# Which engine makes the low parts and scales the softmax rows in two attention stretches

## The chip, the cores and the metric

The kernel runs on one core of a Trainium2 chip. The metric is the device time of one execution in microseconds (us). Engines are called as the profile calls them: PE (TensorE, matmuls), PEld (its weight loads), DVE (VectorE), ACT (ScalarE), POOL (GpSimd), SP (SyncE, which issues most DMAs).

## The reference

Two layers of an encoder over 512 tokens of width 1024, all in float32. Each layer adds to x, in this order, half a gated SwiGLU feed-forward (FFN), a gated mixer, and half a second FFN, each behind an RMS norm with shift and scale from a conditioning vector. The mixer is

```
proj = h @ w_in              # q, k, v of branches A and C, u of B, forget logits, 3 x 1024 gates
ya = attention(qa, ka, va) + learned bias by relative distance, chunk-causal   # 8 heads of 64
yb = (trailing-window means of u - u) @ w_pool * pool_scale                      # windows 2, 4, 8, 16
yc = attention(qc, kc, vc) + cumulative log-forget bias, causal                # 8 heads of 64
out = (sum over n of sigmoid(g_n) * (y_n @ w_branch[n])) @ w_out
```

Softmax is over the keys; q and k are RMS-normalised per head.

## The kernel before, in words

Everything is kept transposed: features on 128 partitions, the 512 tokens along the free dimension. To keep float32 accuracy out of TensorE's faster format (`fp32r`), each operand is split in two: a high part `hi`, which is ScalarE's cast of the value, and a low part `lo`, which is the value minus `hi`. A product is then three matmuls (`triple`, lines 116 to 122): hi by hi, hi by lo, lo by hi.

Weights come in chunks of 512 KB. `wchunk` (from line 241) issues the DMA into `raw` (two buffers), lets ScalarE cast it to `whi` (line 268), and lets VectorE or GpSimd subtract to make `wlo` (line 270; three buffers each). Which engine it is hangs on `lo_share`: where `lo_share[0]` is 0, it is VectorE; where it is n, every n-th chunk goes to GpSimd. The mixer sets it to `LO_SHARE`, which is 1, ahead of branch A's attention and to 0 after branch C's, so that all 48 chunks of these stretches (12 in each of two stretches, in each of two layers) have their low parts made on GpSimd.

The two attention stretches of a layer are written by hand as an interleaving. `attention` walks over 8 heads and, in each, over the 4 blocks of 128 queries. For block i of a head

- `logits` makes the logits of the 128 (i + 1) keys that may be seen (lines 771, 772); VectorE adds the bias strip and takes the maximum (line 775, into a `t1` tile, of which there are two); ScalarE makes the exponentials and their sum (line 779, into one of three `t2` tiles); VectorE takes the reciprocal (line 781) and scales the row (line 782);
- `turn` transposes the scaled row in pieces of 128 on TensorE (line 794); ScalarE casts the high part (line 798) and VectorE makes the low part (line 799);
- `weigh`, once for two blocks, multiplies by v (lines 816, 817), ScalarE and VectorE add the two halves (lines 820, 821, in a `t1` tile), and `split_to` splits the result into the high and low parts of y (lines 370, 371), 64 partitions by 256 columns.

A small planner sets the order: `pe` counts the matmuls issued so far, in units of one matmul of 512 columns; `later(LAG_T, ...)` queues a block's transposes 24 units after its logits, and `later(LAG_V, ...)` queues the weighting 14 units after the last transposes. Between blocks a filler supplies other matmuls, up to a budget of 9.5 or 9 units: in branch A's stretch these are the q, k and v projections of branch C, in branch C's stretch the first merge, which multiplies branch A's y by its weights. So y of branch A is read in branch C's stretch, and y of branch C after it, behind the first product of a gate.

The bias strips (two buffers) are made a head at a time. In branch A a DMA brings the strip, and GpSimd overwrites a corner (line 746). In branch C two DMAs bring it out of DRAM, and GpSimd adds the causal mask to four blocks of 128 columns (line 757), the last of them in a separate tile `ssum` with one buffer. Besides, GpSimd normalises half the rows of q and k (line 659) and clears halves of q's tiles (line 677).

Each engine takes its instructions in order. The order within an engine follows the program's, but the framework that builds the kernel may put an instruction ahead of another that it holds to be ready later.

Of the kernel before, what the change touches and what calls it, by code (L numbers as in the profile page):

```python
# [15 lines left out]
F32 = mybir.dt.float32  # L16
# [3 lines left out]
ALU = mybir.AluOpType  # L20
# [11 lines left out]
NT = T // P  # L32
# [8 lines left out]
def encoder_kernel(tc, xT, c, w_ada, b_ada, gains, w_gate, w_up, w_down, w_qkv, w_f, w_ubg,  # L41
                   qk_gain, rel, fbias, w_pool, pool_scale, w_branch, w_out, inv_cnt, w_first, out):
    nc = tc.nc
# [20 lines left out]
    def st(shape, dt, tag, bufs):  # L64
        return sb.tile(shape, dt, tag=tag, bufs=bufs, name=nm(tag))
# [4 lines left out]
    def mmt(shape=(P, T)):  # L70
        return ps.tile(list(shape), F32, tag="mm", bufs=4, name=nm("mm"))

    def blk(tag, dt=F32R):
        bufs = {"xv": 4, "v2": 4, "b": NB}[tag]
        return st([P, 2, T], dt, tag, bufs)

    def t1(cols=T):
        return st([P, cols], F32, "t1", 2)

    def t2(cols=T):  # L80
        return st([P, cols], F32, "t2", 3)
# [16 lines left out]
    def later(delay, fn, group=None):  # L98
        t = Task(pe[0] + delay, fn, group)
        tasks.append(t)  # L100
        return t

    def poll(everything=False, group=None):
        if polling[0]:
            return
        polling[0] = True
        while True:
            ready = [t for t in tasks if t.fn is None or everything or t.due <= pe[0]
                     or (group is not None and t.group == group)]
            if not ready:  # L110
                break
            t = min(ready, key=lambda z: z.due)
            tasks.remove(t)
            t.run()
        polling[0] = False
# [250 lines left out]
            for d in range(KD):  # L366
                later(STEP * d, lambda d=d: self.pieces[hs].pop(0)() if len(self.pieces[hs]) == KD - d else None)

    def split_to(hi, lo, src):
        nc.scalar.copy(hi, src)  # L370
        nc.vector.tensor_tensor(lo, src, hi.bitcast(F32), op=ALU.subtract)  # L371


    def k_outer(chunk_src, nch, lhs_rhs, before_last=None):
# [57 lines left out]
    class Ffn:  # L432
# [19 lines left out]
        def act(self, n, pg, pu):  # L452
            sg = t1(T)
            nc.scalar.activation(sg, pg, AF.Silu)
            pr = t2(T)
            nc.vector.tensor_tensor(pr, pu, sg, op=ALU.mult)  # L456
            a = blk("b")
            split_to(a[:, 0, :], a[:, 1, :], pr)
            return a
# [164 lines left out]
    def proj_v(l, col, tag, res):  # L624
        vt = [None] * NT

        def evac(t, a):
            b = st([P, H, 2, HD], F32R, tag, 4)
            a3 = a.rearrange("p (h d) -> p h d", h=H)
            for odd in range(2):  # L630
                hi, lo = b[:, odd::2, odd, :], b[:, odd::2, 1 - odd, :]
                split_to(hi, lo, a3[:, odd::2, :])
            vt[t] = b

        yield from proj(l, col, evac)
        res.extend(vt)
# [65 lines left out]
    def finish_turns(upto=3):  # L702

        for todo in turns:
            while len(todo) >= 4 - upto:
                todo.pop(0)()


    def forget(l):
        raw = st([P, KD, H], F32, "wf", 1)  # L710
        nc.sync.dma_start(raw, w_f[l])
        f2 = st([P, KD, 40], F32R, "ssum", 1)
        nc.gpsimd.memset(f2.bitcast(F32), 0.0)
        split_to(f2[:, :, :H], f2[:, :, 32:32 + H], raw)
        pf = mmt()
        for k in range(KD):
# [26 lines left out]
    def strip_a(l, h):  # L743
        s = st([P, 768], F32, "strip", 2)
        nc.sync.dma_start(s[:, :T], rel[l, h])
        nc.gpsimd.memset(s[0:64, T - 64:T], NEG)
        return [s[:, T - (i + 1) * P:T] for i in range(NT)]
# [12 lines left out]
    def attention(qs, ks, vs, strip, ys, filler, budget, group):  # L760


        open_pt = {}

        def logits(h, i, strips):
            p, off = divmod(h, 2)
            (q, ql), k = qs[p], ks[p]
            odd = h % 2
            n = (i + 1) * P
            s = mmt()  # L770
            mm(s[:, :n], q[:, odd, i * P:(i + 1) * P], k[:, odd, :n], start=True, stop=False)
            mm(s[:, :n], ql[:, odd, i * P:(i + 1) * P], k[:, odd, :n], start=False, stop=True)
            lg = t1(T)[:, :n]
            mx = st([P, 1], F32, "mx", 4)
            nc.vector.tensor_tensor_reduce(out=lg, in0=s[:, :n], in1=strips[i], scale=-1.0, scalar=BIG,
                                           op0=ALU.add, op1=ALU.min, accum_out=mx)
            pr = t2(T)[:, :n]
            sm = st([P, 1], F32, "sm", 4)
            nc.scalar.activation(pr, lg, AF.Exp, bias=mx, scale=-1.0, accum_out=sm)
            rs = st([P, 1], F32, "rs", 4)  # L780
            nc.vector.reciprocal(rs, sm)
            nc.vector.tensor_scalar(pr, pr, rs, None, op0=ALU.mult)
            pe[0] += 0.5 * (i + 1.5)
            later(LAG_T, lambda: turn(h, i, pr), group)

        def turn(h, i, pr):
            half, c = divmod(i, 2)
            nj = 2 * half + 2
            if c == 0:
                open_pt[h] = st([P, 2, nj, 256], F32R, "ptb" if half else "pta", 2 if half else 1)  # L790
            pt = open_pt[h]
            tp = mmt()
            for j in range(i + 1):
                nc.tensor.transpose(tp[:, j * P:(j + 1) * P], pr[:, j * P:(j + 1) * P], ident)
            tv = tp[:, :(i + 1) * P].rearrange("p (j q) -> p j q", q=P)
            dh = pt[:, 0, :i + 1, c * P:(c + 1) * P]
            dl = pt[:, 1, :i + 1, c * P:(c + 1) * P]
            nc.scalar.copy(dh, tv)
            nc.vector.tensor_tensor(dl, tv, dh.bitcast(F32), op=ALU.subtract)
            pe[0] += 0.55 * (i + 1)  # L800
            if c == 1:
                later(LAG_V, lambda: weigh(h, half, pt), group)

        def weigh(h, half, pt):
            p, off = divmod(h, 2)
            rows = slice(off * HD, off * HD + HD)
            other = slice(HD - off * HD, 2 * HD - off * HD)
            if off == 0 and half == 0:
                ys.append(blk("b"))
            y = ys[p]  # L810
            o = mmt((P, HALF))
            nj = 2 * half + 2
            for j in range(nj):
                q0 = P if j == nj - 1 else 0
                v2 = vs[j][:, h, :, :].rearrange("p a d -> p (a d)")
                mm(o[:, q0:], v2, pt[:, 0, j, q0:], start=(j == 0), stop=False)  # L816
                mm(o[:, q0:], v2, pt[:, 1, j, q0:], start=False, stop=(j == nj - 1))  # L817
            cols = slice(half * HALF, (half + 1) * HALF)
            yl = t1(T)[:, :HALF]
            nc.scalar.copy(yl[rows, :], o[other, :])  # L820
            nc.vector.tensor_tensor(yl[rows, :], o[rows, :], yl[rows, :], op=ALU.add)
            split_to(y[rows, 0, cols], y[rows, 1, cols], yl[rows, :])
            pe[0] += 1.0 * nj

        for h in range(H):
            strips = strip(h)
            if group == "c":
                finish_turns(h // 2)
            for i in range(NT):
                logits(h, i, strips)  # L830
                if i == NT - 1:
                    heads[0] = h + 1
                poll()
                goal = pe[0] + budget
                while filler is not None and pe[0] < goal:
                    if next(filler, "end") == "end":
                        filler = None
                poll()
        if filler is not None:
            for _ in filler:  # L840
                pass
# [82 lines left out]
    class Mixer:  # L924
# [10 lines left out]
        def run(self, nxt):  # L935
# [14 lines left out]
            def fill_a():  # L950
                yield from proj_qk(l, 3, g8[:, 2:3], True, qc)
                yield from proj_qk(l, 4, g[:, 3:4], False, kc)
                yield from proj_v(l, 5, "v2", vc)
                yield from forget(l)

            lo_share[0] = LO_SHARE
            attention(qa, ka, va, lambda h: strip_a(l, h), ya, fill_a(), FILL_A, "a")
# [62 lines left out]
                    residual_tail(d, hs, o, modc[:, l, 5, d:d + 1], nxt)  # L1020

    FILL_A, FILL_C = 9.5, 9.0
    LO_SHARE = 1

    phases = []
    for l in range(L):
# [64 lines left out]
```

## Time and profile before

| what | value |
|---|---|
| median of 3 runs | 2480.24 us (2478.81 to 2480.9) |
| the profiled execution, span from first to last instruction | 2478.9 us |
| mean granted TensorE clock | 0.998 |
| attention A and C, layer 0 | about 460 to 585 and 585 to 675 us |
| attention A and C, layer 1 | about 1690 to 1810 and 1810 to 1900 us |
| instructions of PE, DVE, ACT, POOL | 11898, 2474, 1634, 327 |

The profiled execution's span lies inside the spread of the three runs, 1.3 us below their median. A row of a group reads: line, engine, operation, output<-inputs, shapes, count | busy us, mean ns of one | idle us before it <- what ended that. A row of the waits reads: who <- for whom: us in total, times, longest. A row of the timeline reads: start, length, engine, line, operation, count, and in brackets the idle time before it. "L782" is line 782.

### The profile page before, as it was taken

The page shows a single profiled execution, that of the slowest core. Times are in us where ns is not written, and L with a number is a line of the kernel's source. Part 1 is how long each engine was busy: PE and PEld are TensorE (multiplying, and loading weights), DVE is VectorE, ACT ScalarE, POOL GpSimd, SP SyncE. Part 2 cuts the span into 40 slices and gives each one's busy share as a digit, 9 for nine tenths or more (in the row PEclk, how much of TensorE's full clock was granted, in tenths as well). Part 3 has the DMA queues.
Part 4 walks back from the last instruction along what each step waited for, and adds up shares of the span by engine and source line. Part 5 has one row for each costly group of instructions (what it writes and reads, how often), then busy time and mean ns, then how long its engine had stood idle before and what let it go on. Part 6 is the DMA issues. An engine that isn't in the chain of part 4 may idle for free. (4 is left out here: it accounts for less than half of the span.)

```text
span 2478.9 us, 30855 instructions
## 1 busy us (share of the span) xinstructions
PE 2425.1 (98%) x11898; PEld 2030.1 (82%) x11898; DVE 1372.2 (55%) x2474; ACT 979.9 (40%) x1634; POOL 340.5 (14%) x327
## 2 busy tenths in 40 slices
PE   7999999999999999999999999999899999999999
PEld 5888888777788898888898888977778888888888
DVE  8655536788753365555365533377787434533332
ACT  5322235676532342222343223366765334432221
POOL 2000002343322200000000000124332322000000
PEclk9999999999999999999999999999999999999999
DMA  7655542222323435555335533322233233223322
GB/s 270 222 198 187 195 136 86 85 73 93 109 90 111 136 110 189 185 204 184 123 109 197 187 119 94 128 92 90 62 107 100 92 119 128 77 94 97 99 94 94
DMA packets 116263, 320.02 MB, mean 129 GB/s; under 512 B 11122, under 2 KB 13298, under 8 KB 116116
## 3 DMA queue, kind: packets, MB, share of 16 engines
q1 hardware_dynamic: 114962, 313.86, 37.9%
q0 software_dynamic: 1152, 4.19, 0.4%
q8 instruction: 93, 1.52, 0.3%
q14 instruction: 54, 0.44, 0.1%
q10 hardware_dynamic: 2, 0.00, 0.0%
HBM read 311.64 MB, written 6.38 MB: 128 GB/s over the span
## 5 line engine op out<-in xcount | busy, mean ns | idle before, releaser
L268 ACT CAST whi<-raw 128x1024 fp32r<-128x1024 f32 (+1 forms) x395 | 411.8, 1045 | 1077.3 <-PE acc L120 412.0
L270 DVE TENSOR_TENSOR wlo<-raw,whi 128x1024 fp32r<-128x1024 f32 x339 | 418.7, 1238 | 516.4 <-ACT whi L268 504.3
L121 PE MATMUL mm<-hhi,wlo 128*128 128x512 f32 x1304 | 507.4, 389 | 0.4 <-DVE wlo L270 0.4
L119 PE MATMUL mm<-hhi,whi 128*128 128x512 f32 x1304 | 507.6, 389 | 0.0
L120 PE MATMUL mm<-hlo,whi 128*128 128x512 f32 x1304 | 507.3, 389 | 0.0
L119 PE MATMUL acc<-b,whi 128*128 128x512 f32 (+1 forms) x960 | 355.9, 371 | 0.0
L121 PE MATMUL acc<-b,wlo 128*128 128x512 f32 (+1 forms) x960 | 353.5, 368 | 0.0
L120 PE MATMUL acc<-b,whi 128*128 128x512 f32 (+1 forms) x960 | 353.4, 368 | 0.0
L121 PEld LDWEIGHTS mm<-hhi,wlo 128*128 128x128 f32 x1304 | 244.8, 188 | 51.4 <-DVE wlo L270 0.9
L119 PEld LDWEIGHTS mm<-hhi,whi 128*128 128x128 f32 x1304 | 245.1, 188 | 50.9
L120 PEld LDWEIGHTS mm<-hlo,whi 128*128 128x128 f32 x1304 | 244.8, 188 | 50.8
L197 DVE CUSTOM_DVE_ANT_0 v<-v,b,badac 128x1024 f32<-128x1024 f32 x144 | 189.2, 1316 | 37.0 <-DMA v<-in_w_ada_dram 36.6
L121 PEld LDWEIGHTS acc<-b,wlo 128*128 128x128 f32 x960 | 181.0, 189 | 29.7
L120 PEld LDWEIGHTS acc<-b,whi 128*128 128x128 f32 x960 | 181.1, 189 | 29.3 <-DVE b L371 0.3
L119 PEld LDWEIGHTS acc<-b,whi 128*128 128x128 f32 x960 | 181.0, 189 | 28.8
L119 PE MATMUL acc<-hhi,whi 128*128 128x512 f32 x480 | 192.3, 402 | 1.7 <-ACT hhi L558 1.7
L121 PE MATMUL acc<-hhi,wlo 128*128 128x512 f32 x480 | 189.7, 395 | 0.6 <-POOL wlo L270 0.5
L120 PE MATMUL acc<-hlo,whi 128*128 128x512 f32 x480 | 188.9, 394 | 1.0 <-DVE hlo L561 1.0
L456 DVE TENSOR_TENSOR t<-mm,t 128x512 f32<-128x512 f32 x86 | 59.4, 691 | 202.7 <-PE mm L121 201.6
L270 POOL TENSOR_TENSOR wlo<-raw,whi 128x1024 fp32r<-128x1024 f32 (+1 forms) x56 | 132.9, 2376 | 170.9 <-ACT whi L268 136.4
L119 PE MATMUL acc<-whi,hhi 128*128 128x512 f32 x336 | 138.3, 412 | 4.9 <-ACT t L648 3.7
L120 PE MATMUL acc<-wlo,hhi 128*128 128x512 f32 x336 | 132.3, 394 | 0.0
(231 smaller groups left out, 3416.8 us busy)
## 6 DMA issues: line engine op xcount, KB each, us to landing
v<-in_w_ada_dram SPq DMA_DIRECT2D x144, 512.0 KB, 4.6
raw<-in_w_down_dram SPq DMA_DIRECT2D x88, 512.0 KB, 3.7
raw<-in_w_up_dram SPq DMA_DIRECT2D x82, 512.0 KB, 3.5
raw<-in_w_gate_dram SPq DMA_DIRECT2D x79, 512.0 KB, 3.6
raw<-in_w_ubg_dram SPq DMA_DIRECT2D x56, 512.0 KB, 3.5
raw<-in_w_qkv_dram SPq DMA_DIRECT2D x42, 512.0 KB, 3.8
raw<-in_w_branch_dram SPq DMA_DIRECT2D x24, 512.0 KB, 3.7
raw<-in_w_out_dram SPq DMA_DIRECT2D x16, 512.0 KB, 3.7
```

The lines of the kernel that those rows point to most:

```text
L119: mm(o, lh, rh, start=start, stop=False)
L120: mm(o, lh, rl, start=False, stop=False)
L121: mm(o, ll, rh, start=False, stop=stop)
L197: dot = nc.vector.tensor_tensor_reduce(out=raw, in0=raw, in1=silc[0], scale=1.0, scalar=badac[:, l, j, d:d + 1], op0=ALU.mult, op1=ALU.add ...
L268: nc.scalar.copy(hi, raw)
L270: lo_eng.tensor_tensor(lo, raw, hi.bitcast(F32), op=ALU.subtract)
L456: nc.vector.tensor_tensor(pr, pu, sg, op=ALU.mult)
```

## The change

In the two attention stretches the low parts of all weight chunks are made on VectorE (`LO_SHARE` is 0, so `lo_share` stays off). The softmax rows of 128, 256 and 384 columns are scaled on GpSimd; those of 512 columns stay on VectorE. The low parts of y in `weigh` are made on GpSimd; the other uses of `split_to` keep VectorE.

```diff
-    def split_to(hi, lo, src):
+    def split_to(hi, lo, src, lo_eng=nc.vector):
         nc.scalar.copy(hi, src)
-        nc.vector.tensor_tensor(lo, src, hi.bitcast(F32), op=ALU.subtract)
+        lo_eng.tensor_tensor(lo, src, hi.bitcast(F32), op=ALU.subtract)
...
             nc.vector.reciprocal(rs, sm)
-            nc.vector.tensor_scalar(pr, pr, rs, None, op0=ALU.mult)
+            (nc.vector if i == NT - 1 else nc.gpsimd).tensor_scalar(pr, pr, rs, None, op0=ALU.mult)
...
-            split_to(y[rows, 0, cols], y[rows, 1, cols], yl[rows, :])
+            split_to(y[rows, 0, cols], y[rows, 1, cols], yl[rows, :], nc.gpsimd)
...
-    LO_SHARE = 1
+    LO_SHARE = 0
```

## The prediction

> **What bounds the kernel now.** I read the page first, then busy time by stretch, then what TensorE waited for, then single collisions in the timeline. The page has the span and each engine's share:
>
> ```profile
> span 2478.9 us, 30855 instructions
> ...
> PE 2425.1 (98%) x11898; PEld 2030.1 (82%) x11898; DVE 1372.2 (55%) x2474; ACT 979.9 (40%) x1634; POOL 340.5 (14%) x327
> ```
>
> TensorE is idle for 2478.9 - 2425.1 = 53.8 us in all, so no change that leaves the matmuls alone can bring more than about 2%. Where is that idle time? The rows by stretch give start and end, length, and then the busy time of PE, PEld, DVE, ACT and POOL. The first two are attention A and attention C of layer 0, the next two those of layer 1, the last is a stretch of FFN:
>
> ```profile
> 460.00:585.00 125.00, 116.07 (x589) 92.24 (x588) 96.33 (x248) 86.83 (x185) 48.80 (x37) 0.99 0.26 80
> 585.00:675.00 90.00, 83.85 (x453) 68.72 (x452) 72.61 (x192) 56.21 (x142) 32.78 (x40) 0.98 0.33 106
> 1690.00:1810.00 120.00, 109.91 (x567) 87.50 (x568) 93.01 (x240) 81.89 (x178) 45.51 (x36) 1.00 0.27 81
> 1810.00:1900.00 90.00, 84.74 (x460) 69.97 (x459) 72.00 (x195) 57.43 (x143) 32.85 (x41) 0.98 0.34 110
> 850.00:1250.00 400.00, 400.00 (x2039) 343.06 (x2039) 220.35 (x354) 128.62 (x179) 17.62 (x17) 1.00 0.46 161
> ```
>
> The FFN stretch has no idle time on TensorE at all. The attention stretches have 8.93 + 6.15 + 10.09 + 5.26 = 30.4 us of it in 425 us, and VectorE is busy there for 333.95 us, 78.6%. What TensorE waited for, summed over the program (total, times, longest):
>
> ```profile
> PE mm L794 <- DVE t L782: 7.2, 7, 2.1
> PE mm L817 <- DVE ptb L799: 5.3, 5, 1.2
> ...
> PE acc L121 <- POOL wlo L270: 0.5, 1, 0.5
> ```
>
> The largest is the transposes of the softmax rows (L794) waiting for the scaling of the rows (L782); then the weighted sums waiting for VectorE's low parts of the transposed rows. GpSimd's low parts of the weight chunks make TensorE wait hardly ever (0.5 us). But see what they do to VectorE. Three rows of the timeline (start, length), GpSimd, VectorE and TensorE:
>
> ```profile
> 606.98 2.35 POOL L270 TENSOR_TENSOR wlo<-raw,whi 128x1024 fp32r<-128x1024 f32 x1
> ...
> 607.19 2.43 DVE L782 TENSOR_SCALAR t<-t,rs 128x512 f32<-128x512 f32 x1
> ...
> 609.68 0.66 PE L794 MATMUL mm<-ident,t 128*128 128x128 f32 x4 [2.10 <-DVE t L782]
> ```
>
> The scaling starts while GpSimd works on a chunk's low part, ends only after it, at 609.62, and the transposes behind it stand still for 2.10 us. The same scaling takes 0.48 us elsewhere (below). So the two engines exclude each other for such operations, and the 2.4 us pieces on GpSimd are paid on VectorE, on the path to TensorE.
>
> **The change part by part.** VectorE's groups, and three single undisturbed instructions:
>
> ```profile
> L270 DVE TENSOR_TENSOR wlo<-raw,whi 128x1024 fp32r<-128x1024 f32 x339 | 418.7, 1238 | 516.4 <-ACT whi L268 504.3
> ...
> L371 DVE TENSOR_TENSOR b<-t,b 64x256 fp32r<-64x256 f32 x64 | 36.6, 572 | 11.1 <-ACT b L370 9.9
> L782 DVE TENSOR_SCALAR t<-t,rs 128x512 f32<-128x512 f32 x32 | 30.6, 956 | 0.8
> ...
> L782 DVE TENSOR_SCALAR t<-t,rs 128x384 f32<-128x384 f32 x32 | 18.9, 592 | 0.8
> L782 DVE TENSOR_SCALAR t<-t,rs 128x128 f32<-128x128 f32 x32 | 18.8, 586 | 0.8
> ...
> L782 DVE TENSOR_SCALAR t<-t,rs 128x256 f32<-128x256 f32 x32 | 11.8, 370 | 0.7
> ```
>
> ```profile
> 478.81 0.41 DVE L371 TENSOR_TENSOR b<-t,b 64x256 fp32r<-64x256 f32 x1
> ...
> 598.84 0.48 DVE L782 TENSOR_SCALAR t<-t,rs 128x512 f32<-128x512 f32 x1
> ...
> 599.98 0.28 DVE L782 TENSOR_SCALAR t<-t,rs 128x128 f32<-128x128 f32 x1
> ```
>
> The groups of 128 columns average 586 ns, more than those of 256 (370): that is no price of the work but of collisions. And GpSimd's groups:
>
> ```profile
> L270 POOL TENSOR_TENSOR wlo<-raw,whi 128x1024 fp32r<-128x1024 f32 x48 | 115.8, 2417 | 136.4 <-ACT whi L268 110.6 <-PE acc L119 17.6 <-issue 8.0
> ...
> L315 POOL TENSOR_TENSOR ssum<-ssum,t 128x256 f32<-128x256 f32 x30 | 22.1, 738 | 98.7 <-ACT t L314 98.6
> L757 POOL TENSOR_TENSOR strip<-strip,cmask 128x128 f32<-128x128 f32 x48 | 21.8, 481 | 76.2 <-DMA strip<-fv_dram 64.1 <-DVE mx L775 8.2 <-DVE pta L799 4.0
> ...
> L160 POOL TENSOR_SCALAR_AFFINE_SELECT cmask<-cmask 128x128 f32<-128x128 f32 x1 | 0.3, 293 | 0.0
> ...
> L159 POOL MEMSET cmask<- 128x128 f32 x1 | 0.2, 204 | 0.0
> ```
>
> *Chunk low parts to VectorE.* 48 x 1.238 = +59.4 us on VectorE, -115.8 us on GpSimd. Each is done 1.2 us sooner once started, and releases its raw buffer sooner; no DMA holds TensorE in the stretches, so that is worth nothing by itself.
>
> *Rows of 128, 256 and 384 columns to GpSimd.* VectorE loses 18.8 + 11.8 + 18.9 = 49.5 us. On GpSimd no such scaling stands in the trace. Upper end: its two-input form, 0.481 us at 128 columns, 0.738 at 256, and by the same slope 0.995 at 384: 2.21 us a head, 71 us for 32 heads. Lower end: the memset's 0.204 us at 128 columns, scaled alike, 0.94 us a head, 30 us. I take the row that is likest, one input, one output, 0.293 us at 128: 0.293 / 0.481 of the upper end, so 0.29, 0.45 and 0.61 us, 1.35 us a head, 43 us. [...]
>
> *Low parts of y to GpSimd.* VectorE loses 36.6 us. GpSimd gains 64 x 0.738 = 47 us (two inputs, 256 columns; half the partitions, which I take not to shorten it). The merges that read y come a stretch later for branch A, and behind a gate's product for branch C; that cover hides some 0.3 us more each. If it were gone the price would be 64 x 0.33 = 21 us. One thing isn't covered by that: the source of y's low part is one of two `t1` buffers which the logits also use, so a late GpSimd would hold up the next logits on VectorE.
>
> *VectorE in sum.* +59.4 - 49.5 - 36.6 = -26.7 us. The 512-column rows stay on VectorE and now pay 32 x (0.956 - 0.48) = 15.2 us in collisions. GpSimd's longest new piece is about 0.74 us where it was 2.4, so I leave a third of that: -10 us more. VectorE's busy time in the four stretches goes from 334 to about 297 us, 78.6% to 69.9%. GpSimd goes to 340.5 - 115.8 + 43 + 47 = 315 us, no bound.
>
> *TensorE's idle time.* Of the 7.2 us behind L782, a 2.4 us blockade shrinks to at most 0.74: I take off 5 us. The other 30.4 - 7.2 = 23.2 us are waits for a VectorE that runs late in its queue. I let them shrink as queueing does, with busy / (1 - busy): 0.786 / 0.214 = 3.67 becomes 0.699 / 0.301 = 2.32, 37% less, 8.6 us. That is an estimate; its bounds are 0 and 23.2.
>
> *What is added.* A GpSimd stage between VectorE's reciprocal and the transposes. How much room is there? A VectorE scaling and its transposes in branch C, and a tight one (the scaling at 599.98 above):
>
> ```profile
> 625.53 0.35 DVE L782 TENSOR_SCALAR t<-t,rs 128x256 f32<-128x256 f32 x1
> ...
> 628.68 0.38 PE L794 MATMUL mm<-ident,t 128*128 128x128 f32 x2
> ...
> 600.52 0.27 PE L794 MATMUL mm<-ident,t 128*128 128x128 f32 x1
> ```
>
> The first ends at 625.88, 2.80 us before it is needed; the second at 600.26, 0.26 us before. Most rows have 2 to 4 us of room, and a longer scaling costs nothing there. I count 20 of the 96 as tight and 0.15 us each, +3 us; below that 0, above it the first rival.
>
> Sum: -5 - 8.6 + 3 = -10.6 us on the profiled span, 2478.9 to 2468.3. The profiled execution lies 1.3 us under the median of the runs, 2480.24, so the forecast is 2469.6 us.
>
> **The rivals.**
>
> *The same exclusion the other way round.* GpSimd now has short urgent work, VectorE long pieces:
>
> ```profile
> 745.71 2.37 POOL L971 TENSOR_TENSOR xv<-xv,t 128x512 f32<-128x512 f32 x1 [6.90 <-DVE t L970]
> ...
> 745.70 1.23 DVE L270 TENSOR_TENSOR wlo<-raw,whi 128x1024 fp32r<-128x1024 f32 x1
> ```
>
> GpSimd's sum starts with VectorE's chunk and ends 2.37 us later, 1.14 us of which remain after VectorE is done: it waited out the chunk. If all 20 tight scalings met a chunk, that is 20 x 1.23 = 25 us against the 13.6 us won: +11, 2491 us. Past 11 meetings (13.6 / 1.23) it is a loss. Against it: 12 chunks of 1.24 us are 15 us of a stretch of 90 to 125 us, so a scaling meets one about one time in seven. Chance 0.07. [...]
>
> *GpSimd's queue stands behind a bias strip.* GpSimd takes its instructions in order, and in branch C it masks each head's strip, which waits for a DMA:
>
> ```profile
> POOL strip L757 <- DMA strip<-fv_dram: 37.3, 7, 8.2
> ...
> 617.50 1.49 POOL L757 TENSOR_TENSOR strip<-strip,cmask 128x128 f32<-128x128 f32 x3 [7.57 <-DMA strip<-fv_dram]
> ```
>
> 37.3 us in 7 waits is 5.3 us each. If a row's scaling is queued behind such a wait, 5.3 - 2.8 = 2.5 us reach TensorE; for 7 heads in each of two layers 35 us, less the 10.6 won: 2504 us. It decides when more than 4 heads are hit so. For it: the order of a queue is made anew when the program is built (at 606.98 above a chunk's low part stands between mask adds that the code issues in a row). Against it: a strip is fetched two heads ahead, so the rows in flight were issued before it. Chance 0.07.
>
> *No change.* A VectorE queue that is stopped by other things:
>
> ```profile
> POOL wlo L270 <- ACT whi L268: 48.2, 9, 12.7
> ```
>
> In the first stretch GpSimd stood 48.2 us waiting for the high parts from ScalarE, at no cost. VectorE takes over that wait, and behind it stand the logits, the low parts of the transposed rows, the reciprocals. If 0.2 to 0.3 us of it are lost on each of 48 chunks, 10 to 14 us, the gain is gone: 2476 to 2484 us. For it: every wait of VectorE lies on TensorE's path. Against: where a chunk stands in the queue is chosen by when its high part should be ready. Chance 0.18.
>
> **How the numbers follow.** Forecast 0.68, no change 0.18, the two slower ones 0.07 each. A measurement of this kernel can tell about 0.2%, 5 us. Low end: three quarters of the 30.4 us gone, 2457. High end: the no-change case, 2484. Beyond lie the slower rivals and little else. Faster 0.68, same 0.18, slower 0.14.
>
> **What would show it.** Right: PE idle in the four stretches near 20 us; VectorE's 512-column scalings below 0.7 us on average; VectorE busy near 297 us there; GpSimd's scalings near 0.3, 0.45 and 0.6 us; no row "PE mm L794 <- POOL t L782" above some 3 us. Wrong: that row large, with GpSimd's own idle time ended by a strip's DMA (the queue) or its scalings stretched beyond 1 us (the exclusion); or logits waiting for VectorE chunks. A gain far above 11 us would mean that idle time was VectorE's lateness nearly alone.

## The result and the profile after

The changed kernel takes 2472.67 us (median of 7 runs, 2471.66 to 2472.94), the kernel before beside it 2480.18 us (7 runs, 2477.77 to 2481.32). The ratio is 0.9973 [0.9962, 0.9983]: 7.5 us or 0.3% faster. The forecast was 2469.6.

The page of the changed kernel:

```profile
span 2470.9 us, 31073 instructions
...
PE 2424.9 (98%) x11898; PEld 2028.9 (82%) x11898; DVE 1328.2 (54%) x2362; ACT 981.6 (40%) x1634; POOL 377.3 (15%) x439
```

The span is 8.0 us shorter. TensorE's busy time is the same (2425.1 before), so nearly all of it is idle time: 2470.9 - 2424.9 = 46.0 us where it was 53.8. The same four attention stretches (start and end, length, then PE, PEld, DVE, ACT, POOL, granted clock):

```profile
455.00:580.00 125.00, 117.22 (x604) 93.26 (x604) 92.46 (x230) 88.50 (x189) 43.63 (x55) 1.00 0.27 79
580.00:670.00 90.00, 85.65 (x461) 69.99 (x460) 59.41 (x167) 58.41 (x146) 51.80 (x75) 0.98 0.35 111
1680.00:1802.00 122.00, 113.89 (x588) 90.59 (x587) 90.00 (x225) 86.13 (x184) 43.49 (x55) 1.00 0.27 80
1802.00:1892.00 90.00, 85.61 (x459) 69.77 (x458) 59.10 (x166) 58.14 (x145) 52.89 (x74) 0.98 0.35 110
```

TensorE's idle time in them is 7.78 + 4.35 + 8.11 + 4.39 = 24.6 us, where it was 30.4 (the four are 427 us long together, 425 before). VectorE is busy for 301 us, where it was 334. What TensorE waits for now (total, times, longest):

```profile
PE mm L794 <- POOL t L782: 7.1, 16, 0.7
...
PE mm L771 <- DVE t L821: 4.5, 6, 1.1
...
PE mm L771 <- DVE ptb L799: 3.2, 2, 1.8
...
PE mm L817 <- DVE ptb L799: 0.7, 2, 0.3
```

The 7.2 us behind VectorE's scalings are gone, and 7.1 us behind GpSimd's scalings stand in their place: 16 short waits of at most 0.7 us where there were 7 of up to 2.1. The weighted sums (L817) wait 0.7 us for the low parts of the transposed rows, where it was 5.3; part of that has moved, since the logits (L771) now wait 3.2 us for the same line. The groups of the moved operations (count | busy us, mean ns | idle before):

```profile
L371 POOL TENSOR_TENSOR b<-t,b 64x256 fp32r<-64x256 f32 x64 | 56.4, 880 | 95.3 <-ACT b L370 94.2
...
L782 POOL TENSOR_SCALAR t<-t,rs 128x384 f32<-128x384 f32 x32 | 39.9, 1248 | 38.3 <-DVE rs L781 32.8 <-PE mm L794 2.8 <-PE acc L121 2.4
...
L782 POOL TENSOR_SCALAR t<-t,rs 128x256 f32<-128x256 f32 x32 | 29.6, 926 | 32.7 <-DVE rs L781 22.7 <-DVE nt_q L282 3.7 <-PE acc L121 3.3
...
L782 POOL TENSOR_SCALAR t<-t,rs 128x128 f32<-128x128 f32 x32 | 19.4, 606 | 66.8 <-DVE rs L781 66.6
...
L782 DVE TENSOR_SCALAR t<-t,rs 128x512 f32<-128x512 f32 x32 | 16.6, 519 | 1.2
```

GpSimd takes 0.61, 0.93 and 1.25 us for a scaling, about twice what was taken for it and more than its two-input form of the same width (0.48 and 0.74 us in the trace of before). VectorE's scalings of 512 columns fell from 956 to 519 ns.

### The profile page after: what moved, and what is told of

Read it like the earlier page. It is cut to its first block, busy times and chain, and to the rows that moved or that the text cites. A ratio compares the mean times of both kernels' runs of the same rounds, so it can differ in the third digit from the quotient of the medians.

```text
span 2470.9 us, 31073 instructions
## 1 busy us (share of the span) xinstructions
PE 2424.9 (98%) x11898; PEld 2028.9 (82%) x11898; DVE 1328.2 (54%) x2362; ACT 981.6 (40%) x1634; POOL 377.3 (15%) x439
## 5 line engine op out<-in xcount | busy, mean ns | idle before, releaser
L270 DVE TENSOR_TENSOR wlo<-raw,whi 128x1024 fp32r<-128x1024 f32 x387 | 478.7, 1239 | 527.2 <-ACT whi L268 514.7
L197 DVE CUSTOM_DVE_ANT_0 v<-v,b,badac 128x1024 f32<-128x1024 f32 x144 | 189.6, 1318 | 37.1 <-DMA v<-in_w_ada_dram 36.8
L121 PE MATMUL acc<-whi,hlo 128*128 128x512 f32 x336 | 132.1, 393 | 0.0
```

The lines of the kernel that those rows point to most:

```text
L121: mm(o, ll, rh, start=False, stop=stop)
L197: dot = nc.vector.tensor_tensor_reduce(out=raw, in0=raw, in1=silc[0], scale=1.0, scalar=badac[:, l, j, d:d + 1], op0=ALU.mult, op1=ALU.add ...
L270: lo_eng.tensor_tensor(lo, raw, hi.bitcast(F32), op=ALU.subtract)
```

## The experiments

Two theories were set against each other. **X, exclusion**: what cost TensorE its time was that VectorE stands still while GpSimd works on a chunk's low part; taking the chunks off GpSimd is the whole gain, and each operation put on GpSimd instead costs something. **L, load**: the gain is that VectorE has less to do, so the moves off VectorE carry it. The diffs of e1 to e3 are against the kernel before, those of e4 and e5 against the changed kernel, those of e8 and e14 against e5, the others against e1. e11 and e12 add one GpSimd operation for each chunk, whose output nobody reads.

### The three parts one by one

**e1_lo_dve**: only the chunks' low parts are moved; the scalings and y's low parts stay on VectorE.

```diff
-    LO_SHARE = 1
+    LO_SHARE = 0
```

> Before, with only the chunks' low parts moved to VectorE (scalings and y's low parts stay there too). [...] Then most of it is here, though VectorE has 59 us more work: 2471 to 2476 us, scalings of 128 columns near 0.29 us, of 512 near 0.49. Theory L, load: the gain comes from the 86 us of work taken off VectorE. Then this kernel, which adds 59 us to VectorE and takes nothing off, is slower than before: 2485 us or more.

Measured: 2454.75 us, ratio 0.9902 [0.9888, 0.9915], 24 us faster than before and 18 us faster than the whole change. Its page and its four stretches:

```profile
PE 2418.0 (99%) x11898; PEld 2027.1 (83%) x11898; DVE 1376.9 (56%) x2522; ACT 979.7 (40%) x1634; POOL 233.1 (10%) x279
```

```profile
453.00:580.00 127.00, 121.54 (x630) 97.33 (x629) 105.17 (x271) 91.32 (x194) 13.17 (x22) 1.00 0.27 84
580.00:670.00 90.00, 88.87 (x495) 74.30 (x494) 75.95 (x218) 62.17 (x156) 17.14 (x33) 1.00 0.35 106
1680.00:1800.00 120.00, 114.10 (x603) 91.40 (x602) 99.77 (x269) 86.59 (x193) 14.57 (x25) 1.00 0.27 81
1800.00:1890.00 90.00, 88.83 (x487) 74.16 (x487) 74.54 (x206) 59.13 (x145) 15.55 (x30) 1.00 0.36 113
```

VectorE is busier than before the change (355 us here, 334 then), and TensorE's idle time is 427.00 - 413.34 = 13.7 us, less than half of the 30.4. That is X and the opposite of L. VectorE's own rows show why:

```profile
L371 DVE TENSOR_TENSOR b<-t,b 64x256 fp32r<-64x256 f32 x64 | 27.9, 436 | 8.7 <-ACT b L370 7.0
...
L782 DVE TENSOR_SCALAR t<-t,rs 128x512 f32<-128x512 f32 x32 | 16.3, 510 | 0.8
...
L782 DVE TENSOR_SCALAR t<-t,rs 128x128 f32<-128x128 f32 x32 | 11.2, 351 | 0.6
```

Without GpSimd's chunks the same instructions take 436 instead of 572, 510 instead of 956 and 351 instead of 586 ns (X had said 0.29 us for the last). The time is 16 us below the range that X gave, 2471 to 2476 us, because X took the gain of the whole change for all there was to win. This kernel beats both others.

**e2_scale_pool**: only the scalings are moved.

```diff
-            nc.vector.tensor_scalar(pr, pr, rs, None, op0=ALU.mult)
+            (nc.vector if i == NT - 1 else nc.gpsimd).tensor_scalar(pr, pr, rs, None, op0=ALU.mult)
```

> Before, with only the rows of 128 to 384 columns scaled on GpSimd; GpSimd keeps the chunks' low parts. X: no gain, rather a loss, since a scaling may stand behind a 2.4 us piece in GpSimd's queue: 2480 to 2490 us, with TensorE waiting for GpSimd's scalings by more than the 7.1 us seen after the change. L: VectorE loses 49.5 us of work, so more than half of the gain: about 2475 us.

Measured: 2471.86 us, ratio 0.9974 [0.9963, 0.9985], 7 us faster. X had no gain here and missed; L, with about 2475 us, came nearer. TensorE's waits:

```profile
PE mm L817 <- DVE pta L799: 6.2, 2, 3.1
...
PE mm L794 <- POOL t L782: 1.8, 4, 0.6
```

The groups that stay on VectorE:

```profile
L371 DVE TENSOR_TENSOR b<-t,b 64x256 fp32r<-64x256 f32 x64 | 46.7, 730 | 11.4 <-ACT b L370 9.9
...
L782 DVE TENSOR_SCALAR t<-t,rs 128x512 f32<-128x512 f32 x32 | 26.7, 834 | 1.8
```

Taking 96 scalings off VectorE takes them out of the collisions with GpSimd's chunks, which go on for the 512-column rows (834 ns here, 510 in e1) and y's low parts (730 ns, 436 in e1). So part of the exclusion can be ended from this side as well; that is a reading within X, found after the run.

**e3_ylo_pool**: only y's low parts are moved (`split_to` takes the engine as in the change; those lines are left out).

```diff
-            split_to(y[rows, 0, cols], y[rows, 1, cols], yl[rows, :])
+            split_to(y[rows, 0, cols], y[rows, 1, cols], yl[rows, :], nc.gpsimd)
```

> Before, with only the low parts of y made on GpSimd. X: the pieces of 2.4 us stay, so little: 2477 to 2481 us. L: VectorE loses 36.6 us of work, 40% of the gain: 2476 to 2477 us.

Measured: 2479.87 us, ratio 1.0006 [0.9997, 1.0015]. Its page:

```profile
PE 2424.3 (98%) x11898; PEld 2029.1 (82%) x11898; DVE 1337.6 (54%) x2410; ACT 979.7 (40%) x1634; POOL 389.4 (16%) x391
```

VectorE has 35 us less to do (1337.6 us busy where it was 1372.2), and the time is the same, as X had it: less load brought no gain here. It isn't a clean test of load, since the move has a price of its own. TensorE's wait for GpSimd's chunks, 0.5 us before the change, is now

```profile
PE acc L121 <- POOL wlo L270: 4.2, 4, 1.3
```

so a gain from the lower load may have been paid back.

### What the two moves to GpSimd cost once the chunks are gone

**e4_lo_scale**: e1 and the scalings, that is, the change without y's low parts.

```diff
-            split_to(y[rows, 0, cols], y[rows, 1, cols], yl[rows, :], nc.gpsimd)
+            split_to(y[rows, 0, cols], y[rows, 1, cols], yl[rows, :])
```

> Chunks' low parts on VectorE and the rows of 128 to 384 columns scaled on GpSimd, as in the change; y's low parts stay on VectorE. The chunks alone gave 2454.75 us, the whole change 2472.67, so one or both of the moves to GpSimd cost 18 us. Theory S: GpSimd's scalings are slow (0.61, 0.93, 1.25 us where VectorE takes 0.28, 0.35, 0.41) and late for the transposes, which waited 7.1 us for them after the change: 2460 to 2466 us. Theory H: it is y's low parts alone that cost: 2453 to 2457 us.

Measured: 2460.52 us, ratio 0.9929 [0.9917, 0.9942], about 6 us slower than e1. TensorE's wait for the scalings in e4 and then in e1:

```profile
PE mm L794 <- POOL t L782: 6.9, 11, 1.9
```

```profile
PE mm L794 <- DVE t L782: 2.6, 9, 0.5
```

The GpSimd stage costs some 6 us, of which 6.9 - 2.6 = 4.3 stand in this wait.

**e5_lo_ylo**: e1 and y's low parts, that is, the change without the scalings.

```diff
-            (nc.vector if i == NT - 1 else nc.gpsimd).tensor_scalar(pr, pr, rs, None, op0=ALU.mult)
+            nc.vector.tensor_scalar(pr, pr, rs, None, op0=ALU.mult)
```

> The change without its scalings: chunks' low parts on VectorE, y's low parts on GpSimd, all rows scaled on VectorE. X: the whole gain and a little more, since the 7.1 us that TensorE waits for GpSimd's scalings after the change fall away: 2468 to 2472 us. L: VectorE has 23 us more work than before the change (59.4 less 36.6), so no gain: 2480 us or more.

Measured: 2472.84 us, ratio 0.9976 [0.9966, 0.9987], 18 us slower than e1, just above X's range and far from L's. X had expected a gain from leaving the scalings out and got none. In the change itself, beside the scalings, the same move costs 2472.67 - 2460.52 = 12 us. So of the change's three parts one brings 24 us and the other two give 17 of them back, mostly y's low parts. The chain by which they do it stands in the timeline of the changed kernel, branch C of layer 0:

```profile
605.22 1.23 DVE L270 TENSOR_TENSOR wlo<-raw,whi 128x1024 fp32r<-128x1024 f32 x1 [0.48 <-ACT whi L268]
...
605.57 1.47 POOL L371 TENSOR_TENSOR b<-t,b 64x256 fp32r<-64x256 f32 x1 [0.69 <-ACT b L370]
...
607.07 0.60 ACT L910 ACTIVATE t<-acc 128x512 f32<-128x512 f32 x1 [0.86 <-POOL b L371]
```

GpSimd's piece starts within VectorE's chunk and ends 0.59 us after it, 1.47 us in all where it takes 0.73 alone: it waited the chunk out. So did 13 of the 64 in all, each ending 0.58 to 0.61 us after its chunk. The piece's source is a `t1` buffer. ScalarE's next gate (line 910) wants that buffer for its output, and stands still until the piece is done; behind it in ScalarE's queue are the exponentials and the high parts of the transposed rows. ScalarE's waits in 580 to 670 us of the changed kernel:

```profile
ACT t L910 <- POOL b L371: 5.8, 3, 2.5
```

The same row has 7.2 us in 1802 to 1892, and 8.4 and 8.6 us in e5. In e1 there is no such wait. It is not the whole story: e3 has 8.7 us of it over the program, in shorter waits (1.6 us at most), and its time is that of the kernel before.

### Is the cost of y's low parts the held buffer?

If it is, a buffer of its own for the source must take it away. The edits make room for it, and a control with y's low parts on VectorE and the same room tells what the room alone does.

**e8_lo_ylo_own** and **e9_lo_own**: the source in a buffer of its own, with GpSimd (e8) and VectorE (e9, the control). Room comes from two constants, one of which is loaded where it is used.

```diff
-            yl = t1(T)[:, :HALF]
+            yl = st([P, HALF], F32, "yl", 1)
...
-    icnt = cp.tile([P, 4, 16], F32, name="icnt")
...
-    apre = cp.tile([P, L, 3, KD], F32, name="apre")
+    apre = gainc
...
+        icnt = st([P, 4, 16], F32, "wf", 1)
+        nc.sync.dma_start(icnt, inv_cnt)
```

> Chunks' low parts on VectorE, y's low parts on GpSimd, but their source in a buffer of its own and no longer in one of the two t1 buffers (room is made by keeping the scaled gains in place of the gains, and by loading the pooling counts when they are used). With t1 the same moves gave 2472.84 us, without y's low parts on GpSimd 2454.75. Theory H, holding: GpSimd's slow piece keeps a t1 buffer, and the logits and gates that need it wait on VectorE and ScalarE: then nearly all comes back, 2454 to 2460 us. Theory P: GpSimd's new two-input pieces of 0.74 us stand in VectorE's way as the chunks' did, or the new order of the queues is a worse one: then little comes back, 2468 to 2473 us.

> Chunks' low parts on VectorE, y's low parts there too, with the buffer of its own for their source: a control for the other kernel with that buffer. H and P: as without that buffer, 2452 to 2457 us.

Measured: 2491.54 us, ratio 1.0055 [1.0042, 1.0067], and 2489.43 us, ratio 1.0045 [1.0031, 1.0059]. Both theories missed. The control is 35 us slower than e1, and not by waiting. The pages of e9 and then of e8:

```profile
PE 2454.1 (99%) x11898; PEld 2026.5 (81%) x11898; DVE 1374.1 (55%) x2522; ACT 979.8 (39%) x1634; POOL 231.8 (9%) x279
```

```profile
PE 2455.0 (99%) x11898; PEld 2027.9 (81%) x11898; DVE 1354.4 (54%) x2458; ACT 979.3 (39%) x1634; POOL 287.5 (12%) x343
```

In e9 TensorE is idle for 2489.1 - 2454.1 = 35.0 us, as in e1 (34.8), but busy for 36.1 us more with the same matmuls. The idle time of the pair can still be compared: in e8 it is 2491.8 - 2455.0 = 36.8 us, 1.8 more than in the control. With `t1` as source the same move took it from 34.8 us (e1) to 2470.2 - 2424.0 = 46.2 us (e5), 11.4 more. That speaks for H, as far as waiting goes. In the FFN stretch 850 to 1250 us, the same group in e9 and then in e1:

```profile
L119 PE MATMUL mm<-hhi,whi 128*128 128x512 f32 x328 | 129.5, 395 | 0.0
```

```profile
L119 PE MATMUL mm<-hhi,whi 128*128 128x512 f32 x328 | 127.6, 389 | 0.0
```

A matmul is modelled 6 ns longer; from start to start they follow each other at a median of 233 ns where it is 227 in e1, everywhere in the FFN. The edit doesn't touch these products, but it moves their operands in memory; the constants that it takes out are 256 and 192 bytes per partition.

**e15_lo_pad**: e1 with an unused tile of 256 bytes per partition ahead of those operands, so a shift the other way.

```diff
+    pad = cp.tile([P, 64], F32, name="pad")
+    nc.gpsimd.memset(pad, 0.0)
```

> Chunks' low parts on VectorE, nothing else but an unused tile of 256 bytes a partition ahead of the tiles that hold the normalised x, so that these and all that lies behind move by 256 bytes. If the place in memory sets the pace of the products: 233 ns between the gate and up matmuls, 2480 to 2495 us. If not: 2453 to 2457 us.

Measured: 2454.36 us, ratio 0.9902 [0.9888, 0.9916], as e1, and 227 ns. This shift does nothing; what makes 233 ns in e8 and e9 stays open.

**e13_lo_own2** and **e14_lo_ylo_own2**: the same pair with the room made elsewhere, and no constant moved (VectorE in e13, GpSimd in e14).

```diff
-            yl = t1(T)[:, :HALF]
+            yl = st([P, HALF], F32, "yl", 1)
...
-        v = st([P, NT * H], F32, "nt_v32", 2)
+        v = st([P, NT * H], F32, "nt_v32", 1)
...
-        raw = st([P, KD, H], F32, "wf", 1)
+        raw = t2(T)[:, :KD * H].rearrange("p (k h) -> p k h", h=H)
...
-        hd = st([P, 16], F32, "hd", 1)
+        hd = t2(T)[:, :16]
```

> Chunks' low parts on VectorE, and a buffer of its own for the source of y's low part, this time with room made behind the large constant tiles, so that these stay where they were; y's low parts on VectorE. The first control with such a buffer was 34.7 us slower than the kernel without it although TensorE waited no longer: its gate and up products came every 233 ns where all other kernels have 227, and its constants lay 256 bytes lower. If the place in memory did that: 2453 to 2458 us here. If the buffer itself does it: about 2489 us.

> The same with y's low parts on GpSimd. With t1 as source, this move cost 18.1 us (2472.84 against 2454.75); with the first buffer of its own 2.1 us (2491.54 against 2489.43). Theory H, holding: 2455 to 2460 us, some 2 us above the kernel beside it. Theory P, GpSimd's pieces in VectorE's way: 2468 us or more.

Measured: 2472.99 us, ratio 0.9979 [0.9970, 0.9988], and 2474.39 us, ratio 0.9980 [0.9971, 0.9989]. With a buffer of its own, y's low parts on GpSimd cost 1.4 us instead of 18. That is what the held buffer would give. But the control itself is 18 us slower than e1, which no theory had, so the pair shows no clean price: e13 has waits of its own, which may hide those of GpSimd (the logits wait 5.0 us for the normalised q and k, line 679, where e1 has 1.9; e9 has the same 5.0).

The traces say more about what the price is not. The chunk waited out does not cost much by itself: in e14 all 14 pieces that overlap a chunk end 0.59 to 0.60 us after it, where in e5 there are 9 such pieces. Nor do GpSimd's pieces stretch VectorE's work by much, the first half of theory P: VectorE's scalings average 311, 349, 452 and 518 ns in e5 and 351, 349, 417 and 510 in e1. And the new buffer is held as well, by a piece that reads it while ScalarE wants to write the next one:

```profile
ACT yl L820 <- POOL b L371: 6.9, 5, 2.4
```

So in both pairs the cost nearly goes when the source leaves `t1`, although it is still held in a buffer: it is the gate's and the logits' use of `t1` that makes it dear. Neither control is as fast as e1, so this is likely and not shown. Left open are what the order of the queues does, which every edit makes anew, and TensorE's busy time, 6.0 us longer in e5 than in e1 (the last section comes back to that).

### Is it really exclusion, and for which operations?

**e11_lo_dummy**: e1, and after each chunk of the stretches a two-input operation on GpSimd, on data that is no longer needed. It takes nothing from VectorE's queue and nobody waits for it but the DMA of the next chunk but one. `in_stretch[0]` is true from the start of branch A's attention to the end of branch C's; the lines that set it are left out.

```diff
+        if in_stretch[0]:
+            nc.gpsimd.tensor_tensor(raw, raw, raw, op=ALU.add)
```

> Chunks' low parts on VectorE, but GpSimd adds each raw chunk of the attention stretches to itself afterwards, in place, a sum of the same size that nobody reads: it brings back GpSimd's 2.4 us pieces and nothing else. Theory X, exclusion: the 24 us are lost again, 2476 to 2485 us, and VectorE's 512-column scalings average over 0.8 us. Rival C: the gain came from having the chunks' low parts 1.2 us sooner, which stays: 2454 to 2458 us.

**e12_lo_dummy_scal**: the same with one input.

```diff
+        if in_stretch[0]:
+            nc.gpsimd.tensor_scalar(raw, raw, 2.0, None, op0=ALU.mult)
```

> As the kernel with the sums that nobody reads (2484.51 us), but GpSimd multiplies each raw chunk by a constant in place, one input instead of two. Theory X with exclusion for every GpSimd piece: 2480 us or more, as pieces get longer (0.61, 0.93 and 1.25 us for 128, 256 and 384 columns make 2.9 us for 1024). If a one-input piece lets VectorE pass (GpSimd's scalings varied by only 6 ns, 602 to 608, next to VectorE's work): 2455 to 2462 us.

Measured: e11 2484.51 us, ratio 1.0028 [1.0016, 1.0039], 30 us slower than e1; e12 2460.67 us, ratio 0.9927 [0.9913, 0.9942], 6 us slower. e11 is in the range of X, e12 in that for one-input pieces that let VectorE pass. In e11 all that e1 won is gone, and some 6 us more, by 48 operations whose output nobody reads. One sign was missed: VectorE's 512-column scalings average 503 ns there, no more than in e1. The collisions fall on the others, 759, 502 and 605 ns for 128, 256 and 384 columns (351, 349 and 417 in e1).

The operations also hold the chunks' raw buffers longer, so the loss could come from late DMAs. It doesn't: SyncE waits for them as long in e12, which loses only 6 us. The row of e11 and then of e12:

```profile
SPq L259 <- POOL raw L274: 249.9, 43, 16.8
```

```profile
SPq L259 <- POOL raw L274: 261.4, 42, 15.4
```

Two pairs of rows of the timeline, first e11, then e12 (line numbers are 4 higher here, 786 is the scaling):

```profile
613.60 2.07 POOL L274 TENSOR_TENSOR raw<-raw 128x1024 f32<-128x1024 f32 x1
...
614.89 0.87 DVE L786 TENSOR_SCALAR t<-t,rs 128x128 f32<-128x128 f32 x1
```

```profile
604.30 2.95 POOL L274 TENSOR_SCALAR raw<-raw 128x1024 f32<-128x1024 f32 x1
...
605.58 0.29 DVE L786 TENSOR_SCALAR t<-t,rs 128x128 f32<-128x128 f32 x1
```

Both scalings start about 1.3 us after GpSimd did. Beside the two-input operation it ends at 615.76, 0.09 us after GpSimd; beside the one-input operation it takes its 0.29 us and is done while GpSimd goes on for 1.38 us. The pairs are typical. In e11 every scaling that began 0.17 to 1.29 us into GpSimd's operation, 26 of them, ended 0.08 to 0.22 us after it. In e12 all 22 that began 0.86 to 1.42 us into it kept their usual length, but of the 20 that began nearer its start or end 16 were held, by 0.1 to 0.8 us. So the full exclusion stands beside GpSimd's two-input work here, and one-input work excluded in part. The traces of the other kernels show the two-input work alike: in the kernel before, all 23 of VectorE's scalings that began 0.08 to 1.86 us into a chunk's low part on GpSimd ended 0.08 to 0.29 us after it, and in the changed kernel the three that began within a y piece, all of 512 columns, ended 0.29 us after it. The scalings that the change puts on GpSimd did VectorE no visible harm: in e4 its low parts of y average 423 ns and its 512-column scalings 515, in e1 436 and 510. Their cost is their own length.

## Why the prediction was right, and where its sizes were off

The direction, the size and the range held: 2472.67 lies 3.1 us above the forecast. The mechanism of the gain was right. That the sum came so close is luck, as the steps show:

- **The bound.** The matmul work didn't move (2425.1 and 2424.9 us), and what was won was idle time, 5.8 of the 7.8 us in the four attention stretches. Right.
- **Chunk low parts to VectorE.** The mechanism read from one timeline triple, that GpSimd's 2.4 us pieces are paid on VectorE, was right: e1 and e11 show it from both sides. The size was not. The terms for it, -5 and -8.6 us, make -13.6; the part alone brings 24 us. The second term went by VectorE's load, and e1, which gains most, adds to that load. The queueing formula gave a plausible number for a wrong reason: VectorE wasn't late because it had much to do, but because single instructions stood still for 1 to 2 us (in e11 such collisions alone bring the lost time back).
- **VectorE in sum.** 297 us were forecast for the four stretches, 301 were measured (over the whole program it fell by 44.0 us, where 36.7 were summed); 512-column scalings below 0.7 us were forecast, 0.52 measured. Right. GpSimd's 315 us came out at 377.3, by the scalings and y's low parts below.
- **Scalings on GpSimd.** 0.29, 0.45 and 0.61 us were taken, with an upper end of 2.21 us a head; measured are 0.61, 0.93 and 1.25, 2.78 us a head, above that end. The upper end was the two-input form, as if one input couldn't cost more than two. Here it did. The 16 waits, 7.1 us in all in the row that was to stay below some 3 us, are the price: 6 us by e4, where +3 was summed. GpSimd's 606 ns at 128 columns stand against 280 for VectorE undisturbed (at 599.98 in the kernel before).
- **Low parts of y on GpSimd.** Summed at nothing, with 21 us as the price if the cover were gone. The reasoning followed the readers of y, which are indeed far away. What it named in its last sentence and gave no price is what happened: the source is held in a `t1` buffer. It was not the logits that felt it most (VectorE waits 3.0 us for it at line 775 in the changed kernel) but the gate on ScalarE (13.0 us at line 910), a third user of these buffers that the prediction had not listed. That the held buffer is what costs is likely by e8 and e14, not shown. The cost is 12 us beside the scalings, 18 without them.
- **Idle in the stretches.** Near 20 us forecast, 24.6 measured.

So the sum of -10.6 came out near -7.5 because two errors offset each other: the good part was worth 10 us more than summed, the two moves to GpSimd cost 14 us more.

**The rivals.** GpSimd waiting out VectorE's chunks was seen, for y's two-input pieces (1.47 us at 605.57 above). For the scalings it was not put to the test: six of them overlap a chunk in the changed kernel, at their usual length (0.93 and 1.25 us), but all six began before the chunk. In e4 two of 384 columns that began beside a 64x256 subtraction of VectorE took 1.50 us where 1.25 is usual. The strip's DMA ahead of a scaling in GpSimd's queue does not appear as a wait of TensorE longer than 0.7 us. VectorE waits for ScalarE's high parts for 7.5 us between 455 and 670 us (14 times, at most 0.9), far from the 48.2 us that GpSimd stood there in the first stretch; e1, with the same chunks on VectorE, is among the fastest kernels. The prediction also said that a gain far above 11 us would mean that idle time was VectorE's lateness nearly alone. e1 has such a gain with a VectorE that is busier, so lateness is not the same as load, which the formula took it for.

## What to carry to other kernels

Look for instructions that take several times their usual length and see what the neighbour engine does at that moment: ending such a collision was worth three times the whole change, while taking 35 us of load off the waiting engine changed nothing on balance (e3). Before a step goes to a slower engine, list who else waits for the buffers that it reads, not only who reads what it writes. A change of several parts should be timed part by part, since a good part can pay for bad ones.

## What the runs showed of the hardware that was not expected

**Short stalls came with a slower clock.** A stretch of the changed kernel, in slices (PE's busy time is the second number, the granted clock the third from the end):

```profile
592.00:594.00 2.00, 1.20 (x9) 0.93 (x8) 0.36 (x1) 0.74 (x2) 1.85 (x4) 1.00 0.48 184
594.00:596.00 2.00, 1.23 (x6) 0.90 (x7) 1.23 (x4) 1.32 (x4) 1.60 (x3) 0.98 0.00 0
596.00:598.00 2.00, 2.00 (x6) 1.51 (x7) 1.57 (x8) 1.28 (x5) 0.52 (x1) 0.50 0.37 131
598.00:600.00 2.00, 2.00 (x11) 1.82 (x10) 0.53 (x3) 1.24 (x4) 1.19 (x3) 0.67 0.00 0
```

TensorE is idle for 0.80 + 0.77 = 1.57 us in 4 us, and then the granted clock is 0.50 for 3.41 us from 595.92 on, which by an estimate from these two numbers costs about 1.7 us more while TensorE counts as busy. What it waited for there, first the sum of two halves for the buffer of the logits, then the maximum, which itself waited for GpSimd's piece of y:

```profile
593.69 0.72 POOL L371 TENSOR_TENSOR b<-t,b 64x256 fp32r<-64x256 f32 x1
...
594.12 0.33 PE L771 MATMUL mm<-b,b 128*128 128x128 f32 x1 [0.91 <-DVE t L821]
...
594.45 0.69 DVE L775 CUSTOM_DVE_ANT_0 t<-mm,ssum 128x512 f32<-128x512 f32 x1 [0.39 <-POOL b L371]
...
595.21 0.38 PE L771 MATMUL mm<-b,b 128*128 128x256 f32 x1 [0.65 <-DVE mx L775]
```

The kernel before has three such pulses, the changed one two, e1, e4, e12 and e15 none: their mean granted clock is 1.000, and their TensorE is busy for 2418.0 to 2418.9 us against 2424 to 2428 in the others of the usual pace. So 7.1 us of e1's gain lie in busy time, where the prediction had looked for nothing. By the same estimate three pulses of 3.41 us at half the clock are 5.1 us of that, the rest is not accounted for. The same goes for y's low parts: of their 12 us in the change, 6.1 are busy time (2424.9 against 2418.8 us in e4). e13 has the most:

```profile
588.00:592.00 4.00, 3.13 (x13) 2.28 (x13) 3.78 (x16) 3.26 (x11) 1.49 (x3) 0.59 0.01 2
592.00:596.00 4.00, 3.71 (x17) 3.31 (x17) 2.62 (x8) 1.99 (x6) 0.00 (x0) 0.50 0.33 94
596.00:600.00 4.00, 3.67 (x19) 3.23 (x17) 2.02 (x6) 1.41 (x5) 1.28 (x3) 0.63 0.01 4
```

Its TensorE is busy for 2427.7 us, 9.7 more than in e1, about half of what its span is longer (2472.6 against 2452.8 us). In the changed kernel the longest gap of TensorE between 592 us and the pulse at 596 us was 0.91 us. That the stalls set off the pulses is read from their order in time; no run tested it.

**Which operations excluded each other.** GpSimd's pieces of y waited out VectorE's chunks in the changed kernel, two inputs on both sides (13 pieces ended 0.58 to 0.61 us after the chunk). In e11 a one-input scaling of VectorE waited out GpSimd's two-input sum (it ended 0.09 us after it). Beside one input on GpSimd's side it was otherwise, in e12: a scaling in the middle of GpSimd's 2.95 us was not delayed (0.29 us at 605.58); only some that started near GpSimd's beginning or end were (one of 128 columns took 0.69 us at 492.74). What makes this difference no run shows.

**GpSimd's one-input scaling is slower than its two-input sum**: 606 and 926 ns at 128 and 256 columns against 481 and 738 (the changed kernel and the kernel before).

**The pace of matmuls** changed by 2.6% (227 to 233 ns) with an edit that doesn't touch them, in e8 and e9; the cause was not found.
